# A state-space branch's diagonal part with two heads side by side, its other parts turned into the same bank

## The chip, the cores and the metric

The kernel runs on one core of a Trainium2 chip, in one launch. The metric is the device time of one execution in microseconds; the number shown for a kernel is the median over its runs. Beside the timed runs there is one profiled execution, from which every instruction's start and length on each engine are known. The engines are named as in the profile: PE multiplies matrices (PEld is its loading of the operand that stays in the array), DVE is the vector engine, ACT the scalar engine, POOL the general one, and SP issues DMAs. All operands are 32 bits wide. A tile of PSUM, into which PE writes, is a bank of 128 partitions by 512 numbers.

## The reference

One layer of a diffusion backbone over 512 latent tokens of width 1024, with 256 context tokens ahead of it. An adaLN-modulated RMSNorm feeds one combined input projection, whose columns go to two parallel mixers (a bidirectional state-space scan, and windowed attention with context keys) and to two gates. Each branch is projected to the model's width, the two are merged under the gates, projected once more and added to the stream; then comes a gated feed-forward part with a convolution. The part that the change touches is the scan's output, per chunk of 128 tokens and per direction:

```
cb = einsum('bclgn,bcsgn->bgcls', cc, bc)
scores = cb[:, :, None] * exp(segsum(ac))
y_diag = einsum('bgrcls,bcsgrp->bclgrp', scores, xc)
y_off = einsum('bclgn,bcgrpn,bgrcl->bclgrp', cc, states[:, :-1], exp(cs))
y = y_diag + y_off
...
y = y + d_skip * xs
return rmsnorm(y * silu(z), g)
```

There are 32 heads of 64 channels in 4 groups of 8 heads, and 4 chunks; the state has 128 numbers per channel. The norm runs over all 2048 channels and is followed by the projection with `w_o_ssd`.

## The kernel before

The kernel is written with a framework that places semaphores and buffers. Within a stretch it keeps the engines' instructions near program order; inside `manual_schedule` they stand exactly in it. The stages follow one another: modulation and the first columns of the gates (to about 64 us), keys, first queries and values (to 104), attention with z columns and further products beside it, in an order that a planner works out (to about 377), the state-space branch (to about 746), output projections (to about 905), and the feed-forward part (up and down products). Products of large weights are taken in three passes of split operands (`gemm`, L187); the branch's own small products are taken in plain 32-bit form, which is two matmuls each.

**The branch** (L1232 to L1509) is a list of steps, `prog`, that `run` (L167) goes through. For each of the 4 groups of heads there are the steps of `ssd_steps(g)` and, between them, projection steps of the next group (`proj_steps(g + 1)`), whose large products fill PE; for the last group the steps between are gate products (`g_step`). `run` loads each step's weights one step ahead.

- `proj_steps` (L1272): the group's B, C and four x tiles, each from a product with the latent tokens and mostly one with the context, then convolution and silu on ACT and DVE. Tiles that must be turned wait in a list, and the next step turns them between its two products (`turn`, L1262): a bank of PSUM per tile, transposes on PE, a copy out on ACT.
- `states` (L1365): the context's states and the backward states. Their pieces are put into the large products (`BETWEEN`).
- `chunk_in(c)` (L1404): loads two blocks of cumulated decays, multiplies C with B (`cb`, L1418), and makes `E`, the decayed scores of 8 heads, in two halves of four: ACT writes the backward part into a bank `eb` (L1436), DVE merges it into the forward part (L1437), ACT takes the exponential, DVE multiplies with `cb` (L1439). `E` lies with source tokens on partitions and output tokens along the free dimension.
- `chunk_out(c)` (L1442): C times the forward and the backward state (L1448), scaled on DVE (L1450) into `parts`. Then the diagonal part: one product per head into its 64 columns of the bank `yd` (L1454), with `E` staying in the array and 64 columns of `xs` streaming, so that tokens are on partitions. POOL adds up the skip term and the two parts in `dx` (L1459 to L1461), DVE adds `yd` and `dx` into `y` (L1462). Then the forward state advances (L1357 to L1360).
- `gate_rows` (L1466), just before the group's last `chunk_in`: loads four tiles of 128 channels by 512 tokens of silu(z), which attention had written to `zs_d`.
- `gate` (L1472), after the last chunk: for each of the four channel tiles, four transposes of `y` into a bank (L1479), a product with the gate rows on DVE (L1480), a store to `yz_d`. The rows' squares are summed for the norm during the next group (`square`, L1323).

In the branch all small products share one pool of five PSUM banks (`misb`, L1229): C times state (two), `yd`, the state's advance, `cb`, two `eb`, turned tiles, the gate's transposes.

**Modulation steps** (`m_step`, L543): the second half of the modulation (w_mod, 32 pieces of 512 KB) isn't multiplied on PE. Each step does two multiply-adds of 128 x 512 on DVE (L554 to L556), and each fourth step ends with four transposes on PE and a sum on DVE (L564 to L567), or for the last two with one product with ones and a sum (L559, L560). Steps 0 to 3 stand around the values' step at L688, steps 4 to 11 in the branch, two per group, 12 to 23 among the output projections, and 24 to 31 woven among the 22 up steps (L2021).

**After the branch**, `y_split` (L1521) loads the 16 tiles of `yz_d` again, multiplies by the norm's weights and splits them into high and low halves for the product with `w_o_ssd` (`os_first`, L1561, for the first two output tiles, pieces os 0 to 3; `os_step` for the others, two pieces each). `load` (L154) casts a weight piece into one of two buffers for the high and two for the low halves, unless `ELSEWHERE` names another place. The last up step takes its second bank from `misb`; then the banks are laid out anew as one pool of eight (`one_pool`, L2005), and the down products begin (L1868).

Products that are only 32 columns wide stand at L359 and L417, in the modulation: their outputs lie in 32 partitions each, four (three) after one another in one bank.

Of the kernel before, what the change touches and what calls it, by code (L numbers as in the profile page):

```python
# [9 lines left out]
F32 = mybir.dt.float32  # L10
# [34 lines left out]
def tile_hybrid_layer(  # L45
# [641 lines left out]
    msteps = [m_step(i) for i in range(32)]  # L687
    run([q_step(1)] + msteps[0:2] + [([("v", i) for i in range(3)], v_step)] + msteps[2:4])  # L688
# [547 lines left out]
    bp = bpool.enter_context(tc.tile_pool(name="bpool", bufs=1, reuse_waits="tile"))  # L1236

# [102 lines left out]
    def ssd_steps(g):  # L1340
# [24 lines left out]
        def states():  # L1365
# [36 lines left out]
            d["y"] = bp.tile([P, 4, 512], F32, tag="y", name="y", bufs=1)  # L1402
# [39 lines left out]
        def chunk_out(c):  # L1442
            xs, y, coef = d["xs"], d["y"], d["coef"]
# [8 lines left out]
            yd = misb()  # L1452
            for h in range(8):
                T.matmul(  # L1454
                    yd[:, h * 64 : (h + 1) * 64], d["E"][h // 4][:, h % 4, :], xs[:, c, h * 64 : (h + 1) * 64],
                    start=True, stop=True,
                )
            dx = bp.tile([P, 512], F32, tag="tf", name="dx", bufs=1)
# [3 lines left out]
            V.tensor_tensor(y[:, c, :], yd, dx, ALU.add)  # L1462
# [3 lines left out]
        def gate_rows():  # L1466
            for ct in range(4):
                zt = bp.tile([P, L], F32, tag="zs", name="zs", bufs=4)
                nc.sync.dma_start(zt, zs_d[4 * g + ct])
                d.setdefault("zt", []).append(zt)  # L1470

        def gate():  # L1472
            y = d["y"]
            if g == 0:
                dump("y", y[:, 1, :])
            for ct, yz in enumerate(d["zt"]):
                ps = misb()
                for c in range(4):
                    T.transpose(ps[:, c * P : (c + 1) * P], y[:, c, ct * P : (ct + 1) * P], ident)  # L1479
                V.tensor_tensor(yz, ps, yz, ALU.mult)  # L1480
                nc.sync.dma_start(yz_d[4 * g + ct], yz)
                SQUARES.append(yz)
                if g == 3:
                    square(False)

        r = [([], states)]
        for c in range(4):
            r += [([], lambda c=c: chunk_in(c)), ([], lambda c=c: chunk_out(c))]
        r[7] = [], lambda f=r[7][1]: (gate_rows(), f())
        return r + [([], gate)]  # L1490

    prog = proj_steps(0)
    for g in range(4):
# [3 lines left out]
        m = msteps[4 + 2 * g : 6 + 2 * g]  # L1497

        prog += s[0:1] + f + b[0:1] + s[1:2] + m[0:1] + b[1:2]
        for c in range(4):  # L1500
            prog += s[2 + 2 * c : 4 + 2 * c] if c < 3 else s[8:9]
# [3 lines left out]
            if c == 1:  # L1505
# [606 lines left out]
```

## Time and profile before

| | before |
|---|---|
| median of 3 runs | 1255.09 us (1254.44 to 1257.48) |
| the profiled execution's own time | 1254.76 us |
| its span, first to last instruction | 1253.0 us |
| PE / PEld busy | 1228.1 / 1010.6 us |
| DVE / ACT / POOL busy | 922.4 / 683.4 / 166.9 us |
| PE's granted clock, mean | 0.996 |

A row of the timeline gives start, length, engine, line, operation, output and inputs, the part of the array that is used (128*128 is all of it), shape, and how many instructions were merged; in brackets stands idle time of the engine just before, and what ended it. A group row gives busy time, mean length in ns, idle time before, and its releasers. PE's matmuls are pipelined: a row's length reaches to the end of the last matmul's way through the array, and the next matmul starts before that.

### The profile page before, as it was taken

Reading aid. Unit: us, or ns where it says so; the run is one execution under the profiler, and the core shown is the slowest. Engines: PE = TensorE matmul, PEld = TensorE weight load, DVE = VectorE, ACT = ScalarE, POOL = GpSimd, SP = SyncE. Lnnn points to the kernel's source line nnn. Section 1 sums busy time; section 2 is a strip of 40 time slices with the busy share of each in tenths; the row PEclk is TensorE's granted clock in tenths of the full one; section 3 lists DMA queues with packets and bytes.
Section 4 is the critical chain, followed back from the end, with each engine's and each line's share of the span. In section 5 each row is a group of like instructions: output and inputs, shape, how many; then the busy total and the mean of one; then the engine's idle time right before and its main releaser. Section 6 shows DMA issues by size and latency. Waiting matters only on the chain. (4 is left out here: it accounts for less than half of the span.)

```text
span 1253.0 us, 17432 instructions
## 1 busy us (share of the span) xinstructions
PE 1228.1 (98%) x6292; PEld 1010.6 (81%) x6292; DVE 922.4 (74%) x1517; ACT 683.4 (55%) x1286; POOL 166.9 (13%) x173
## 2 busy tenths in 40 slices
PE   7999999999999999999999999999999999999997
PEld 4698888888878878788778777888988888887885
DVE  4775888888664688788877767667678888886566
ACT  3566887788544456476565655223545444444543
POOL 0000111112100033242352520000200000000000
PEclk9899999999999999999999999999999999999999
DMA  9573568967946234345365549667145444458785
GB/s 340 220 214 103 185 191 202 227 177 197 245 146 206 74 115 123 126 129 174 112 143 175 160 154 308 219 220 235 58 143 168 152 134 151 149 165 276 228 308 184
DMA packets 109494, 226.74 MB, mean 181 GB/s; under 512 B 9568, under 2 KB 48800, under 8 KB 109408
## 3 DMA queue, kind: packets, MB, share of 16 engines
q1 hardware_dynamic: 101920, 199.42, 49.3%
q0 software_dynamic: 6912, 25.17, 8.6%
q8 instruction: 49, 0.80, 0.3%
q10 hardware_dynamic: 576, 1.05, 0.2%
q14 instruction: 37, 0.30, 0.1%
HBM read 194.34 MB, written 50.92 MB: 196 GB/s over the span
## 5 line engine op out<-in xcount | busy, mean ns | idle before, releaser
L150 DVE TENSOR_TENSOR wlo<-wraw,whi 128x1024 fp32r<-128x1024 f32 (+2 forms) x121 | 152.7, 1262 | 64.8 <-ACT whi L149 61.9
L193 PE MATMUL acc<-hlh,whi 128*128 128x512 f32 x488 | 200.1, 410 | 0.0
L196 PE MATMUL acc<-hlh,wlo 128*128 128x512 f32 x488 | 191.3, 392 | 0.0
L194 PE MATMUL acc<-hll,whi 128*128 128x512 f32 x488 | 190.8, 391 | 0.0
L149 ACT CAST whi<-wraw 128x1024 fp32r<-128x1024 f32 (+2 forms) x121 | 124.9, 1034 | 119.5 <-PE acc L194 72.3
L193 PE MATMUL acc<-mh,whi 128*128 128x512 f32 x360 | 140.6, 390 | 0.0
L194 PE MATMUL acc<-ml,whi 128*128 128x512 f32 x360 | 140.1, 389 | 0.0
L196 PE MATMUL acc<-mh,wlo 128*128 128x512 f32 x360 | 140.1, 389 | 0.0
L196 PEld LDWEIGHTS acc<-hlh,wlo 128*128 128x128 f32 x488 | 91.6, 188 | 20.1
L194 PEld LDWEIGHTS acc<-hll,whi 128*128 128x128 f32 x488 | 91.9, 188 | 18.1 <-issue 2.4
L193 PEld LDWEIGHTS acc<-hlh,whi 128*128 128x128 f32 x488 | 91.9, 188 | 17.7 <-issue 2.4
L194 PEld LDWEIGHTS acc<-ml,whi 128*128 128x128 f32 x360 | 67.6, 188 | 14.2 <-issue 0.2
L193 PEld LDWEIGHTS acc<-mh,whi 128*128 128x128 f32 x360 | 67.6, 188 | 14.1 <-issue 0.2
L196 PEld LDWEIGHTS acc<-mh,wlo 128*128 128x128 f32 x360 | 67.6, 188 | 14.1
L794 DVE CUSTOM_DVE_ANT_0 p<-score,winm,nsink 128x512 f32<-128x512 f32 (+1 forms) x64 | 51.9, 810 | 16.2 <-PE score L785 14.7
L801 ACT ACTIVATE p<-p,mneg 128x512 f32<-128x512 f32 (+1 forms) x64 | 49.7, 777 | 16.9 <-DVE mneg L794 16.4
L1240 DVE SCALAR_TENSOR_TENSOR ta<-acc,half,ta 128x511 f32<-128x511 f32 (+1 forms) x66 | 43.8, 663 | 18.9 <-ACT ta L1239 18.8
L1239 ACT ACTIVATE ta<-acc,half 128x512 f32<-128x512 f32 (+1 forms) x66 | 46.6, 705 | 20.4 <-PE acc L196 19.1
L193 PE MATMUL acc<-hch,whi 128*128 128x256 f32 x176 | 54.4, 309 | 0.0
L829 DVE TENSOR_TENSOR ptl<-pt,pth 128x512 fp32r<-128x512 f32 x72 | 47.5, 685 | 8.5 <-ACT pth L825 7.7
L1359 POOL TENSOR_TENSOR st<-st,eT 128x512 f32<-128x512 f32 x24 | 28.5, 1186 | 177.5 <-ACT st L1376 158.6
L556 DVE SCALAR_TENSOR_TENSOR tm<-wraw,csil,tm 128x512 f32<-128x512 f32 x56 | 41.9, 748 | 11.0 <-DMA wraw<-wm 10.1
(477 smaller groups left out, 2960.7 us busy)
## 6 DMA issues: line engine op xcount, KB each, us to landing
wraw<-wup SPq DMA_DIRECT2D x44, 512.0 KB, 3.8
wt_d<-wdn POOLq DMA_DIRECT2D x36, 512.0 KB, 7.7
wraw<-wm SPq DMA_DIRECT2D x32, 512.0 KB, 3.6
fb<-cs_d SPq DMA_DIRECT2D x32, 512.0 KB, 5.6
wraw<-wx SPq DMA_DIRECT2D x24, 512.0 KB, 3.7
wraw<-wt_d SPq DMA_DIRECT2D x20, 512.0 KB, 4.5
sp_d<-te SPq DMA_DIRECT2D x33, 256.0 KB, 2.4
wm<-wm SPq DMA_DIRECT2D x16, 512.0 KB, 8.0
```

The source lines that it names most:

```text
L149: S.copy(hi[:, :n], r[:, :n])
L150: V.tensor_tensor(lo[:, :n], r[:, :n], raw(hi[:, :n]), ALU.subtract)
L193: T.matmul(ps, wh, xh[:, k0 + k, :], start=a, stop=False)
L194: T.matmul(ps, wh, xl[:, k0 + k, :], start=False, stop=False)
L196: T.matmul(ps, wl, xh[:, k0 + k, :], start=False, stop=b)
L556: V.scalar_tensor_tensor(acc, r[:, u * 512 : u * 512 + 512], sc, acc, ALU.mult, ALU.add)
L794: V.tensor_tensor_reduce(p[:, :w], d["ps"][i][:, o0 : o0 + w], m, op0=ALU.add, op1=ALU.min, scale=1.0, scalar=nsink[:, h : h + 1], accum_o ...
L801: S.activation(p, p, AF.Exp, bias=d["mneg"][:, i : i + 1], scale=-1.0, accum_out=d["den"][:, i : i + 1])
L829: V.tensor_tensor(d["ptl"][x], d["pt"][x], raw(d["pth"][x]), ALU.subtract)
L1239: S.activation(o[:, :n], ps[:, :n], AF.Identity, scale=hcol(base_w, stride + i), bias=hcol(base_b, i))
L1240: V.scalar_tensor_tensor(o[:, 1:n], ps[:, 0 : n - 1], hcol(base_w, i), o[:, 1:n], ALU.mult, ALU.add)
L1359: G.tensor_tensor(h8(n), h8(s), bc64(eT[:, z0 : z0 + 8, c]), ALU.mult)
```

## The change

Seven things are changed.

1. The diagonal part is taken the other way round: 64 columns of `xs` stay in the array and a head's `E` (128 columns) streams, so that channels come out on partitions. The outputs of an even and an odd head lie in partitions 0 to 63 and 64 to 127 of the same 128 columns of a bank `yb`.
2. DVE no longer adds `dx`. A new step `chunk_sum(c)`, which stands after the next projection step (for the last group's first three chunks after the next `chunk_out` and `chunk_in`), turns the four column blocks of `dx` with PE and adds them into the same bank.
3. `chunk_sum` then multiplies the bank with the chunk's columns of the gate rows, in place in `z`, a tile for all four channel tiles with two buffers, loaded at the start of the group in `states`. `gate` has only the stores and the squares left; the tile `y` is gone.
4. The last group's rows aren't stored and loaded again: `y_split` reads them from `z`.
5. Modulation steps 0 to 3 move from the values' step into the branch, which then has three per group; the last eight are woven among the first 20 up steps instead of all 22.
6. The halves of weight piece os 4 go into a buffer of the pool of `z` instead of the common ones.
7. For odd chunks of the last group `dx` lies in another buffer.

```
-    msteps = [m_step(i) for i in range(32)]
-    run([q_step(1)] + msteps[0:2] + [([("v", i) for i in range(3)], v_step)] + msteps[2:4])
+    run([q_step(1), ([("v", i) for i in range(3)], v_step)])
...
+    zpool = ExitStack()
+    zp = zpool.enter_context(tc.tile_pool(name="zpool", bufs=1, side="right", reuse_waits="tile"))
...
-            d["y"] = bp.tile([P, 4, 512], F32, tag="y", name="y", bufs=1)
+            d["z"] = zp.tile([P, 4, L], F32, tag="z", name="z", bufs=2)
+            for ct in range(4):
+                nc.sync.dma_start(d["z"][:, ct, :], zs_d[4 * g + ct])
...
-            yd = misb()
+            yb = misb()
             for h in range(8):
                 T.matmul(
-                    yd[:, h * 64 : (h + 1) * 64], d["E"][h // 4][:, h % 4, :], xs[:, c, h * 64 : (h + 1) * 64],
-                    start=True, stop=True,
+                    yb[64 * (h % 2) : 64 * (h % 2) + 64, h // 2 * P : h // 2 * P + P],
+                    xs[:, c, h * 64 : (h + 1) * 64], d["E"][h // 4][:, h % 4, :],
+                    start=h < 2, stop=False, skip_group_check=True,
                 )
-            dx = bp.tile([P, 512], F32, tag="tf", name="dx", bufs=1)
+            dx = tmp("tc") if g == 3 and c % 2 else bp.tile([P, 512], F32, tag="tf", name="dx", bufs=1)
+            d["y", c] = yb, dx
...
-            V.tensor_tensor(y[:, c, :], yd, dx, ALU.add)
             if c < 3:
                 d["Sf"] = advance(d["Sf"], 0, c, weigh_in(0, c))

-        def gate_rows():
+        def chunk_sum(c):
+
+            yb, dx = d.pop(("y", c))
             for ct in range(4):
-                zt = bp.tile([P, L], F32, tag="zs", name="zs", bufs=4)
-                nc.sync.dma_start(zt, zs_d[4 * g + ct])
-                d.setdefault("zt", []).append(zt)
+                z = slice(ct * P, (ct + 1) * P)
+                T.matmul(yb[:, z], dx[:, z], ident, start=False, stop=ct == 3, is_transpose=True, skip_group_check=True)
+            z = d["z"][:, :, c * P : (c + 1) * P]
+            V.tensor_tensor(z, yb.rearrange("p (a b) -> p a b", a=4), z, ALU.mult)

         def gate():
-            y = d["y"]
...
-            for ct, yz in enumerate(d["zt"]):
-                ps = misb()
-                for c in range(4):
-                    T.transpose(ps[:, c * P : (c + 1) * P], y[:, c, ct * P : (ct + 1) * P], ident)
-                V.tensor_tensor(yz, ps, yz, ALU.mult)
-                nc.sync.dma_start(yz_d[4 * g + ct], yz)
+            for ct in range(4):
+                yz = d["z"][:, ct, :]
                 SQUARES.append(yz)
-                if g == 3:
+                if g < 3:
+                    nc.sync.dma_start(yz_d[4 * g + ct], yz)
+                else:
                     square(False)
+            F["z"] = d["z"]
...
-        m = msteps[4 + 2 * g : 6 + 2 * g]
+        m = msteps[3 * g : 3 * g + 3]
...
         for c in range(4):
-            prog += s[2 + 2 * c : 4 + 2 * c] if c < 3 else s[8:9]
+            prog += s[3 * c + 2 : 3 * c + 3] + (s[3 * c + 4 : 3 * c + 5] if c < 3 else [])
+            if g == 3 and c:
+                prog += s[3 * c : 3 * c + 1]
             prog += b[2 + c : 3 + c]
             if c == 1:
                 prog += b[6:]
-            if c == 1:
-                prog += m[1:2]
-        prog += s[9:10]
+            if g < 3 or c == 3:
+                prog += s[3 * c + 3 : 3 * c + 4]
+            if c in (1, 2):
+                prog += m[c : c + 1]
+        prog += s[13:14]
...
-            t = tmp("ta") if k < 3 else ldt[k % 3] if k % 6 < 3 else cp.tile([P, L], F32, tag="ld", name="ld", bufs=3)
-            nc.sync.dma_start(t, yz_d[k])
+            if k < 12:
+                t = tmp("ta") if k < 3 else ldt[k % 3] if k % 6 < 3 else cp.tile([P, L], F32, tag="ld", name="ld", bufs=3)
+                nc.sync.dma_start(t, yz_d[k])
+            else:
+                t = F["z"][:, k - 12, :]
...
+    def second_piece():
+        t = zp.tile([P, 2, 1024], F32R, tag="z", name="z", bufs=2)
+        return t[:, 0, :], t[:, 1, :]
+
+    ELSEWHERE["os", 4] = second_piece
...
-        + weave([up_step(t) for t in range(NFF)], msteps[24:])
+        + weave([up_step(t) for t in range(NFF - 2)], msteps[24:])
+        + [up_step(t) for t in range(NFF - 2, NFF)]
```

More of the change, by code (lines that the diff above doesn't have):

```diff
@@ L1442, in chunk_out @@
         def chunk_out(c):
-            xs, y, coef = d["xs"], d["y"], d["coef"]
+            xs, coef = d["xs"], d["coef"]
             tok = slice(c * P, (c + 1) * P)
@@ L1712, in close_c1 @@
         c1pool.close()
+        zpool.close()
         c2 = F["c2"] = ctx.enter_context(tc.tile_pool(name="c2pool", bufs=1, reuse_waits="tile"))
```

6 lines of the change are left out of this document (2 added, 4 removed).

## The prediction

> **What bounds the kernel now.** I read the page's busy shares first, then the list of PE's waits, then the busy time of each engine over the branch's first group (window from, to, length; then PE, PEld, DVE, ACT, POOL), then the timeline of PE around the diagonal part.
>
> ```profile
> PE 1228.1 (98%) x6292; PEld 1010.6 (81%) x6292; DVE 922.4 (74%) x1517; ACT 683.4 (55%) x1286; POOL 166.9 (13%) x173
> ```
>
> ```profile
> PE mis L1267 <- DVE y L1462: 0.5, 1, 0.5
> ```
>
> ```profile
> 440.00:506.00 66.00, 65.90 (x363) 52.93 (x362) 56.11 (x89) 42.83 (x105) 25.36 (x17) 1.00 0.37 111
> ```
>
> PE is busy for 98% of the span, and in that group for 65.90 of 66.00 us; DVE, next, has 56.11. So an edit is worth what it takes off PE's own stream, plus the few places where PE stands still. An edit on DVE, ACT, POOL or a queue counts only if it uncovers PE.
>
> **The diagonal part.** Here are one chunk, the group of all sixteen, and the one place where the kernel before already puts products side by side in the array: the modulation products, 32 columns wide, four across.
>
> ```profile
> 467.80 1.88 PE L1448 MATMUL mis<-st,CT 128*128 128x512 f32 x4
> 469.51 1.89 PE L1454 MATMUL mis<-xs,E 128*128 128x64 f32 x16
> 471.25 1.08 PE L1357 MATMUL mis<-xw,Bk 128*128 128x512 f32 x2
> ```
>
> ```profile
> L1454 PE MATMUL mis<-xs,E 128*128 128x64 f32 x256 | 31.1, 274 | 0.7 <-DVE E L1439 0.7
> ```
>
> ```profile
> 13.80 0.84 PE L408 MATMUL mis<-ah,w0l 128*128 128x512 f32 x2
> 14.58 1.07 PE L359 MATMUL acc<-wm,csil 128*32 128x256 f32 x16
> 15.58 0.73 PE L408 MATMUL mis<-ah,w0h 128*128 128x512 f32 x2
> 16.15 0.62 PE L408 MATMUL mis<-al,w0h 128*128 128x512 f32 x2
> ```
>
> ```profile
> L193 PE MATMUL acc<-mh,whi 128*128 128x512 f32 x360 | 140.6, 390 | 0.0
> ```
>
> ```profile
> 14.57 0.59 PEld L359 LDWEIGHTS acc<-wm,csil 128*32 128x32 f32 x16 [0.44 <-issue]
> ```
>
> A product of f32 operands is two matmuls, so eight heads are 16 matmuls. Now they take 471.25 - 469.51 = 1.74 us, 0.109 each. The operand that streams is only 64 wide: four matmuls of 512 columns take 469.51 - 467.80 = 1.71, or 0.428 each, and 64 columns by that are 0.054. So PE is held by the loading of E, 128 columns per matmul. Over all chunks the group is 31.1 busy + 0.7 idle, less 0.15 sixteen times (a row of 1.89 whose successor starts after 1.74): 29.4 us.
>
> After the change xs is loaded (64 columns) and E streams (128 columns, 0.107 by the same rate), with even heads in the left half of the array and odd heads in the right. If the halves run at once, a chunk is 8 x 0.107 = 0.86. What entering and leaving a divided array costs, I take from the modulation row. The second L408 matmul before it starts at 13.80 + 0.84 - 0.39 = 14.25 (0.39 is one matmul of 512 such columns, by the group row; a pair of 0.62 says that they come 0.23 apart); the next was due at 14.48. Afterwards two L408 matmuls precede 16.15, so with no loss they would have begun at 16.15 - 2 x 0.23 = 15.69. That is 1.21 for 16 matmuls of 256 columns, four at once: 4 x 0.214 = 0.86. The visit costs 0.35 beside its streaming. I take 0.86 + 0.35 = 1.21 per chunk, 19.4 in all: **-10.0 us**. Ends: no cost of the visit, 13.8 (-15.6); halves that don't overlap, 16 x 0.107 + 0.35 = 2.06 per chunk, 33.0 (+3.6). I stay near the row of the divided array, since it is the same element type and the same bank for all quarters.
>
> The 16 transposes per group stay 16, only of dx instead of y and four per chunk:
>
> ```profile
> L1479 PE MATMUL mis<-ident,y 128*128 128x128 f32 x64 | 7.6, 272 | 0.0
> ```
>
> ```profile
> 477.86 0.82 PE L1267 MATMUL mis<-ident,tc 128*128 128x128 f32 x6
> ```
>
> Each lasts 0.27, and in a run of only six they come (0.82 - 0.27) / 5 = 0.11 apart, all that their 128 columns stream for, so making four runs of four out of one run of sixteen costs nothing.
>
> **DVE in the branch.**
>
> ```profile
> L556 DVE SCALAR_TENSOR_TENSOR tm<-wraw,csil,tm 128x512 f32<-128x512 f32 x56 | 41.9, 748 | 11.0 <-DMA wraw<-wm 10.1
> ...
> L1462 DVE TENSOR_TENSOR y<-mis,dx 128x512 f32<-128x512 f32 x16 | 11.1, 692 | 24.6 <-POOL dx L1461 24.6
> L1480 DVE TENSOR_TENSOR zs<-mis,zs 128x512 f32<-128x512 f32 x16 | 10.4, 682 | 1.0 <-PE mis L1479 1.0
> ```
>
> The sums of L1462 go: 11.1 busy, and the 24.6 for which DVE stood in front of them for POOL, with the next chunk's E queued behind. The gate products stay 16 of 128x512. Four modulation steps come in: 8 x 0.75 = 6.0, and by the group's 11.0 idle for 56, some 1.6 of waiting for their 512 KB rows. DVE gains near 28 us here, so I cost the steps at nothing; E also comes sooner. With L1462 gone, the 0.5 that L1267 waited goes: **-0.5**. The gate rows' 16 loads move on SP from chunk 3 to the group's start, past the weight loads, and those wait only if a row buffer (two groups deep) is still being squared; the last group's 4 stores and 4 loads go. PE waits for none of these loads: nothing. Were that cover gone, a weight load would come late by one landing of 256 KB, 2.4 us, once per group at most:
>
> ```profile
> sp_d<-te SPq DMA_DIRECT2D x33, 256.0 KB, 2.4
> ```
>
> **The places where PE stands.**
>
> ```profile
> 103.92 0.60 PE L564 MATMUL mis<-ident,tm 128*128 128x128 f32 x4
> 105.60 0.39 PE L785 MATMUL score<-khi,q 128*128 128x256 f32 x1 [1.08 <-DVE mod L566]
> ```
>
> ```profile
> 771.75 1.05 ACT L149 CAST whi<-wraw 128x1024 fp32r<-128x1024 f32 x1 [1.99 <-PE acc L194]
> ...
> 775.45 1.22 DVE L150 TENSOR_TENSOR wlo<-wraw,whi 128x1024 fp32r<-128x1024 f32 x1
> ...
> 776.72 0.50 PE L196 MATMUL acc<-yh,wlo 128*128 128x512 f32 x1 [1.67 <-DVE wlo L150]
> ```
>
> ```profile
> 1133.34 1.02 PE L559 MATMUL mis<-tm,ones 128*128 128x512 f32 x2
> ...
> 1135.01 0.68 DVE L560 TENSOR_TENSOR g<-mis,g 128x512 f32<-128x512 f32 x1
> 1135.61 0.74 DVE L1762 SCALAR_TENSOR_TENSOR tc<-mis,vec,tc 128x511 f32<-128x511 f32 x1
> 1135.84 0.47 PE L1868 MATMUL acc<-ww,fyh 128*128 128x512 f32 x1 [1.48 <-DVE g L560]
> ```
>
> Front: the first score waits 1.08 for the modulation step's bank (L566). That step leaves; its four transposes (0.44) are paid in the branch instead. Next late is the evacuation of the v banks, running since 102. I take **-1.1** (ends -1.1 and 0).
>
> Output weights: the piece for os 4 can be cast only when os 1's buffer is free (771.75), and its low half stands on DVE behind the merges, until 776.67; PE waits 1.67. In buffers of its own both halves can be made as soon as the piece has landed: **-1.7** (ends -1.7, and 0 if DVE keeps its order).
>
> Down: PE waits 1.48 for the last modulation step's bank. Two up steps earlier that step (its 0.85 on PE too) is out of the way, but the last up product's bank is then read until about 1135.7 by L1762 instead. If the first down bank is that one, the wait stays and the 0.85 comes on top; if the second, six matmuls run first and some 1.0 of waiting is left; else it is gone. With one of five banks for each of the first two: 0.2 x 0.85 - 0.2 x 0.5 - 0.6 x 1.5 = **-0.8** (ends -1.5, +0.85).
>
> New waits: the diagonal's bank is now held through the following projection until chunk_sum's product, in a pool of five in which that step turns two tiles and E holds three:
>
> ```profile
> 477.94 0.73 DVE L1437 COPY_PREDICATED E<-sel,mis 128x512 f32<-128x512 uint8 x1
> ...
> 479.97 0.74 DVE L1437 COPY_PREDICATED E<-sel,mis 128x512 f32<-128x512 uint8 x1
> ```
>
> With the turn at 477.86, cb, both E banks and the two turned tiles are five; the held bank is a sixth. The second tile starts at 478.30 and would wait for the first copy, done at 478.67. In this chunk L1462 came before that copy and had waited for POOL 1.19, which goes, so I take the copy as early enough, mostly: **+1.0** over the 12 projection steps (ends 0 and +8.9, below).
>
> Sum: -10.0 - 0.5 - 1.1 - 1.7 - 0.8 + 1.0 = -13.1. The profiled execution took 1254.76 (span 1253.0 and 1.8 around it): 1241.7. The median of the runs, 1255.09, is 0.3 above: **1242.0**. A measurement can tell some 0.3%, 3.8 us, from no change.
>
> **The rivals.**
>
> In order: the two halves start strictly in the program's order, so a head's second pass holds up its neighbour and a chunk is nine rounds, +0.107 x 16 = 1.7: 1243.7. Against it:
>
> ```profile
> 32.85 0.41 PE L417 MATMUL acc<-w,s 128*32 128x256 f32 x3
> 32.89 0.40 PE L359 MATMUL acc<-wm,csil 128*32 128x256 f32 x1
> 33.00 0.48 PE L417 MATMUL acc<-w,s 128*32 128x128 f32 x3
> ```
>
> L417's products all stand ahead of L359's in the program, yet one of L359, in the fourth quarter, starts at 32.89 before the last of L417 at 33.00. The Trainium skill, "TensorE: Matmul & The Clock Gate", Part 3, says that matmuls start and end strictly in program order; by that rule the time would be this rival's, and these rows disagree with it. 6%.
>
> Loads not hidden: each half loads, then streams. One load lasts 0.106 for 32 columns and 0.19 for 128:
>
> ```profile
> L359 PEld LDWEIGHTS acc<-wm,csil x128: 106/110/178, 6.2 to 53.2; 128*32 128x32 f32 x128
> ```
>
> ```profile
> L1454 PEld LDWEIGHTS mis<-xs,E x256: 186/192/192, 456.5 to 738.2; 128*128 128x128 f32 x128
> ```
>
> Between them 64 columns are 0.134, and 8 x (0.134 + 0.107) + 0.35 = 2.28 per chunk, 36.5: +7.1 in place of -10.0, so 1259.1, **slower**. It decides once a load's exposed part passes 0.08. The 16 loads of the modulation row, done within 0.59 while its matmuls run 1.07, speak against it. The same Part 3 says that loads overlap running matmuls only in other row groups, which would make this rival right here; the row disagrees. 5%.
>
> No overlap of the halves: +3.6 in place of -10.0 gives 1255.6, no change. The four quarters at 14.58 speak against it. 6%.
>
> Banks, short: the 0.37 above (478.67 - 478.30) at each turn, and as much again at the next chunk's C product, which needs the held bank's successor: 12 x 0.74 = 8.9 in place of 1.0, 1249.9. For it: the five banks are all taken at 477.86. 8%.
>
> Banks, long: the second turned tile is given the bank of E's second copy, done at 480.71: 2.4 x 12 = 28.9 in place of 1.0, 1269.9, slower. It decides from 1.5 per turn. 5%.
>
> **How the numbers follow.** The forecast has the other 70%. Faster: 70 + 6 + 8 = 84%; same: 6%; slower: 5 + 5 = 10%. The range runs from the visit without cost (-15.6 for -10.0: 1236.4, rounded to 1236.5) up to the short bank waits, 1250.0; outside are 16% in rivals and little below.
>
> **What would show it.** Right: the diagonal as 128*64 matmuls of 128x128, about 1.2 us per chunk from its first start to the next group's; no L1462 among DVE's groups; PE's waits at the score, at os 4's low half and at the first down product gone or smaller; turns of a tile with no idle time before them. Wrong: chunks of over 1.8 us; PE waiting at the turns for a copy of E or for ACT; E late at the diagonal, at more than the 0.7 of before.

## The result and the profile after

| | before | after |
|---|---|---|
| median of 8 runs each | 1255.55 us (1253.54 to 1257.48) | 1251.16 us (1249.31 to 1252.82) |
| the profiled execution's own time | 1254.76 us | 1249.31 us |
| its span | 1253.0 us | 1247.3 us |
| PE / DVE busy | 1228.1 / 922.4 us | 1220.3 / 919.5 us |

The ratio is 0.9965, 95% interval 0.9954 to 0.9976: 4.4 us faster where 13.1 were forecast. The profiled execution after is the fastest of its eight; of the 5.7 by which the spans differ, 1.0 was there before the first product of the gates, ahead of every edited step.

The diagonal came out as forecast. The timeline of PE after, for the chunk of the prediction (start, length, then the operation), and its group:

```profile
463.89 0.60 PE L1475 MATMUL mis<-ident,dx 128*128 128x128 f32 x4
464.32 1.88 PE L1451 MATMUL mis<-st,CT 128*128 128x512 f32 x4
466.14 1.09 PE L1457 MATMUL mis<-E,xs 128*64 128x128 f32 x16
467.16 1.12 PE L1358 MATMUL mis<-xw,Bk 128*128 128x512 f32 x2
468.12 0.38 PE L1421 MATMUL mis<-CT,BT 128*128 128x128 f32 x2
```

```profile
L1457 PE MATMUL mis<-E,xs 128*64 128x128 f32 x256 | 17.9, 280 | 0.3 <-DVE E L1442 0.2
```

From the first start to the next group: 467.16 - 466.14 = 1.02, where it was 1.74. The group ahead lasts 1.82 in place of 1.71 and the one behind 0.96 in place of 0.91, so the visit to the divided array costs 0.16 more around it: 1.18 per chunk against the forecast 1.21, 0.56 saved, 9 us in all. The front's wait and the down product's wait are gone too; the first score and the first down product have no bracket now:

```profile
102.89 0.28 PE L784 MATMUL score<-khi,q 128*128 128x256 f32 x1
...
1130.53 0.39 PE L1885 MATMUL acc<-ww,fyh 128*128 128x512 f32 x1
```

What was not forecast is in the list of PE's waits (us in total, times, longest). In the branch the kernel before had, beside the 0.5 that the prediction shows:

```profile
PE mis L1454 <- DVE E L1439: 0.7, 2, 0.4
PE mis L1267 <- DVE tc L1248: 0.3, 1, 0.3
```

After the change these lines are new or longer:

```profile
PE acc L193 <- ACT whi L149: 2.5, 1, 2.5
PE acc L196 <- DVE wlo L150: 1.2, 1, 1.2
PE mis L1451 <- ACT xs L1311: 1.2, 1, 1.2
PE mis L1268 <- DVE tc L1249: 1.0, 2, 0.8
PE mis L1268 <- DVE E L1440: 0.9, 2, 0.7
...
PE mis L1358 <- DVE z L1477: 0.7, 1, 0.7
```

The last four lie in the branch, where the list now adds up to 4.5 us (0.7 of it in three short lines) and to 1.5 before. The first two lie where the branch ends. The timeline of PE there:

```profile
743.54 0.39 PE L196 MATMUL acc<-hlh,wlo 128*128 128x512 f32 x1
746.43 0.50 PE L193 MATMUL acc<-yh,whi 128*128 128x512 f32 x1 [2.50 <-ACT whi L149]
...
748.37 0.50 PE L196 MATMUL acc<-yh,wlo 128*128 128x512 f32 x1 [1.21 <-DVE wlo L150]
...
749.18 0.63 PE L196 MATMUL acc<-yh,yh 128*128 128x512 f32 x1
749.60 0.63 PE L193 MATMUL acc<-yh,whi 128*128 128x512 f32 x1
```

PE stands for 2.50 and 1.21 us, and then its matmuls of 512 columns come 0.42 to 0.43 apart instead of 0.23. The brackets are somewhat short: they count from the end of the row before, so where 743.54 is followed by 746.43, 2.89 later in place of 0.23, the loss is 2.66. The windows of those stretches (after the length: busy PE, PEld, DVE, ACT, POOL, then the granted clock) show why:

```profile
746.00:749.00 3.00, 1.36 (x5) 0.84 (x6) 3.00 (x4) 1.81 (x3) 0.00 (x0) 1.00 0.98 328
749.00:752.00 3.00, 3.00 (x9) 2.37 (x8) 1.15 (x2) 0.00 (x0) 0.00 (x0) 0.53 0.79 263
```

The granted clock fell to 0.53; it was 1.00 throughout there before. (A window from 749.16 to 752.57 has exactly 0.50: 3.41 us at half speed, which is 1.7 lost.) And this is what ACT did meanwhile, which PE waited for, the cast of weight piece os 0 (L149, at 745.35):

```profile
736.14 2.93 ACT L1536 ACTIVATE yh<-ld,vec 128x512 fp32r<-128x512 f32 x4 [1.21 <-DMA ld<-yz_d]
...
742.55 1.93 ACT L1536 ACTIVATE yh<-ld,vec 128x512 fp32r<-128x512 f32 x3
744.72 0.72 ACT L1536 ACTIVATE yh<-ld,vec 128x512 fp32r<-128x512 f32 x1 [0.24 <-DMA ld<-yz_d]
745.35 1.03 ACT L149 CAST whi<-wraw 128x1024 fp32r<-128x1024 f32 x1
```

In the kernel before, the same cast had stood ahead of the squares and of all the splits (L1526 there):

```profile
743.85 1.05 ACT L149 CAST whi<-wraw 128x1024 fp32r<-128x1024 f32 x1 [5.80 <-PE acc L194]
...
747.63 1.94 ACT L1526 ACTIVATE yh<-ta,vec 128x512 fp32r<-128x512 f32 x3
```

After the change it stands behind the first twelve of the gated rows' splits (L1536), in the order of ACT's queue. The piece's load was issued at 716.60, and the product whose buffer the cast takes over was done at 737.8, before L1475 turns the last chunk.

Where the time went is best read by comparing the start of the same matmul in two timelines, stage by stage. Each number is how much longer (+) or shorter (-) the stage took than in the kernel before, in us of the profiled executions; the front begins at the first product of the gates (63.58 in the kernel before), and the stages end there at 106.18 (first gate product after the scores), 391.98, 745.54 (start of the last gate product), 781.84 (behind the first two output tiles and piece os 4), 1135.84 (first down product) and 1253.0.

| kernel | front | attention | branch | first output tiles | output, up | down |
|---|---|---|---|---|---|---|
| the change | -1.8 | -0.5 | -4.1 | +4.0 | -1.9 | -0.4 |
| e1 stored | -1.8 | -0.4 | -2.6 | +3.3 | -1.9 | -0.4 |
| e2 seam split | -1.8 | -0.4 | -0.5 | -1.9 | -1.9 | -0.3 |
| e3 six banks throughout | -1.8 | -0.4 | -7.0 | +4.9 | +4.3 | -0.4 |
| e4 steps in front | 0.0 | -0.4 | -7.7 | -1.9 | -1.9 | +1.0 |
| e5 second and third step earlier | -1.8 | -0.5 | -2.0 | -1.9 | -1.9 | +0.1 |
| e6 none in last group | -1.8 | -0.4 | -5.7 | -1.9 | -1.4 | -0.4 |
| e7 four steps later | -1.8 | -0.4 | -7.5 | -1.9 | +1.5 | -0.4 |
| e8 heads' order | 0.0 | -0.4 | -2.9 | -1.9 | -1.9 | -0.4 |
| e9 one step late | 0.0 | -0.5 | -7.0 | +4.5 | +0.8 | +1.3 |
| e10 six banks in the branch | -1.8 | -0.4 | -6.1 | +4.5 | -1.9 | +0.7 |
| e11 three in front | -1.8 | -0.4 | -4.6 | -1.9 | -1.9 | +0.3 |
| e12 three in front, six banks | -1.8 | -0.4 | -9.6 | -1.9 | -1.9 | +0.2 |
| e13 steps moved alone | -1.8 | 0.0 | +3.2 | +0.9 | -2.4 | 0.0 |
| e14 without two edits | 0.0 | -0.5 | -7.7 | -2.1 | -2.3 | +0.2 |

So the change lost in two places: in the branch it gained 4.1 of the 9 that its diagonal is worth, and at the first output tiles it lost 4.0, though os 4's wait of 1.67, in the same stage, is gone: 5.7 in all, which is the two waits with what their brackets leave out (2.66 and 1.37) and the 1.7 of the clock.

### The profile page after: what moved, and what is told of

It is laid out like the page before. It is cut to its first block, busy times and chain, and to the rows that moved or that the text cites. A ratio compares the mean times of both kernels' runs of the same rounds, so it can differ in the third digit from the quotient of the medians.

```text
span 1247.3 us, 17416 instructions
## 1 busy us (share of the span) xinstructions
PE 1220.3 (98%) x6292; PEld 994.3 (80%) x6292; DVE 919.5 (74%) x1501; ACT 685.9 (55%) x1286; POOL 164.1 (13%) x173
## 4 chain that ended last, share of the span: by engine, by line
PE 83%; DVE 10%; ACT 2%; issue 2%; DMA 2%; POOL 1%; SPq 0%; POOLq 0%; DVEq 0%; ACTq 0%
PE acc L196 17%; PE acc L193 17%; PE acc L194 17%; PE acc L1887 3%; PE acc L1885 3%; PE acc L1886 3%; PE score L784 3%; PE po L833 3%; PE pt L820 2%; PE mis L408 2%; DVE wlo L150 1%; PE acc L903 1%; PE acc L905 1%; PE acc L904 1%; PE mis L1375 1%
## 5 line engine op out<-in xcount | busy, mean ns | idle before, releaser
L150 DVE TENSOR_TENSOR wlo<-wraw,whi 128x1024 fp32r<-128x1024 f32 (+2 forms) x120 | 149.9, 1250 | 70.0 <-ACT whi L149 61.8
L193 PE MATMUL acc<-hlh,whi 128*128 128x512 f32 x488 | 200.2, 410 | 0.0
L149 ACT CAST whi<-wraw 128x1024 fp32r<-128x1024 f32 (+2 forms) x120 | 123.9, 1034 | 117.6 <-PE acc L194 78.1
L193 PE MATMUL acc<-mh,whi 128*128 128x512 f32 x360 | 141.0, 392 | 0.0
L193 PEld LDWEIGHTS acc<-hlh,whi 128*128 128x128 f32 x488 | 91.8, 188 | 18.3 <-issue 2.9
L193 PEld LDWEIGHTS acc<-mh,whi 128*128 128x128 f32 x360 | 67.6, 188 | 14.5 <-issue 0.5
L193 PE MATMUL acc<-hch,whi 128*128 128x256 f32 x176 | 54.4, 309 | 0.0
L556 DVE SCALAR_TENSOR_TENSOR tm<-wraw,csil,tm 128x512 f32<-128x512 f32 x56 | 44.5, 794 | 13.3 <-DMA wraw<-wm 12.8
```

Source lines behind the costliest of these rows:

```text
L149: S.copy(hi[:, :n], r[:, :n])
L150: V.tensor_tensor(lo[:, :n], r[:, :n], raw(hi[:, :n]), ALU.subtract)
L193: T.matmul(ps, wh, xh[:, k0 + k, :], start=a, stop=False)
L556: V.scalar_tensor_tensor(acc, r[:, u * 512 : u * 512 + 512], sc, acc, ALU.mult, ALU.add)
```

## The experiments

Each is timed beside the kernel before on the same chip, and ratios are to that kernel. The chip isn't the same one for all, so it is the ratios that compare one experiment with another. "The change" is 0.9965.

| kernel | median us | ratio, 95% interval |
|---|---|---|
| e1 | 1248.63 | 0.9963 (0.9951 to 0.9976) |
| e2 | 1246.49 | 0.9936 (0.9923 to 0.9948) |
| e3 | 1253.73 | 0.9991 (0.9982 to 1.0001) |
| e4 | 1241.75 | 0.9903 (0.9889 to 0.9916) |
| e5 | 1246.64 | 0.9929 (0.9916 to 0.9941) |
| e6 | 1241.88 | 0.9901 (0.9886 to 0.9916) |
| e7 | 1243.44 | 0.9906 (0.9892 to 0.9919) |
| e8 | 1245.71 | 0.9928 (0.9915 to 0.9942) |
| e9 | 1253.12 | 0.9984 (0.9973 to 0.9995) |
| e10 | 1248.16 | 0.9952 (0.9939 to 0.9966) |
| e11 | 1242.45 | 0.9907 (0.9893 to 0.9920) |
| e12 | 1238.54 | 0.9873 (0.9859 to 0.9886) |
| e13 | 1254.22 | 0.9999 (0.9990 to 1.0008) |
| e14 | 1241.72 | 0.9893 (0.9879 to 0.9906) |

The first theory was that the end of the branch suffers because the last group's stores are gone from SP; its rival, that the held bank costs what is missing.

**e1: the last group's rows stored and loaded again.**

```
-                if g < 3:
-                    nc.sync.dma_start(yz_d[4 * g + ct], yz)
-                else:
+                nc.sync.dma_start(yz_d[4 * g + ct], yz)
+                if g == 3:
                     square(False)
...
```

> The change as it is, but the last group's four gated tiles are stored and loaded again like the others. Seam theory (without those four stores on SP the split of the gated rows is issued and worked off ahead of os 0's weight piece, so that PE runs dry for 2.50 + 1.21 us at the end of the branch and then gets a lower clock): the old order comes back, PE runs on from the last gate projection into the first output product without idle time, and the time falls by 4 to 6 us below the change, to about 1246. Bank theory (the shortfall is PE's waiting in the branch for a bank that the diagonal holds): the seam is indifferent, within 1 us of the change, about 1251. Prediction's step (those stores and loads are worth nothing): about 1251 too.

The ratio is that of the change, and PE still waited 1.77 and 1.34 us at the first output products. The theory in this form falls: removing those stores and loads is not what made the stall.

**e2: eight of the sixteen splits put behind the first output products.**

```
-        [([], lambda: y_split(range(12)))]
-        + fill[n3:]
-        + [os_first(0), ([], lambda: y_split(range(12, 16))), os_first(1)]
+        [([], lambda: y_split(range(4)))]
+        + fill[n3:]
+        + [([], lambda: y_split(range(4, 8))), os_first(0), ([], lambda: y_split(range(8, 16))), os_first(1)]
```

> The change as it is, but only tiles 0 to 3 of the gated rows are split ahead of the last gate projection, 4 to 7 behind it, 8 to 15 behind os 0 and os 2; stores and loads stay away. Seam theory: os 0's cast comes before the last splits, the wait of 2.50 at the first output product goes, 4 to 6 us below the change, about 1246. Bank theory: within 1 us of the change.

The stall is gone, and the stage of the first output tiles went from +4.0 to -1.9: 5.9 us, as expected for the order of ACT's queue. But the branch, which the edit doesn't name, kept only 0.5 of its 4.1, so the median shows half of it. Its list of waits in the branch is 2.5 us longer than the change's: for turned tiles (DVE tc, 2.5 in place of 1.0) and for E (two lines, 1.0 more). Why DVE is later there I didn't find out.

**e3 and e10: six banks for the branch's products, two for its projections**, throughout (e3), or in the branch alone (e10, which has the second part of the edit too).

```
-    psum_pools(mis=(5, 1), acc=(3, 1))
+    psum_pools(mis=(6, 1), acc=(2, 1))
...
     run(prog)
+    psum_pools(mis=(5, 1), acc=(3, 1))
     bpool.close()
```

> The change with six banks for the branch's products and two for the projections, in place of five and three. Bank theory: PE's waits in the branch for a copy of E, a turned tile or the gate product (0.9, 1.0, 1.0 and 0.4 us in the change) go, 2 to 3 us below the change, about 1248.5, unless two projection banks bring waits of their own at the projections (then slower, and those waits show in the list at the projection matmuls). Seam theory: the wait of 2.50 at the end of the branch stays; no more than 1 us gained. Modulation theory (the waits come from four more modulation steps on DVE): waits stay, no gain.

> The change with six banks for the branch's products and two for its projections, put back to five and three when the branch ends. Bank theory: the branch gains some 2.9 us as it did with six and two throughout, and the output and feed-forward stages lose nothing now: 2 to 3 us below the change, 1248 to 1249. Place theory: the waits at the end of the branch (2.50 and 1.21) stay, and the 5.8 us there. If the gain in the branch was chance, 1251.

The branch gained 2.9 and 2.0 more than in the change. The list of PE's waits of e10 in the branch has lost the gate product's lines and the turns' wait for a copy of E, and has a new one for the two projection banks (L193):

```profile
PE acc L193 <- DVE ta L1242: 1.5, 2, 1.0
PE mis L1268 <- DVE tc L1249: 1.2, 3, 0.9
...
```

In e3 the output stages then lost 6.2 with two banks (+4.3 for -1.9), more than the branch had won; e10 keeps its gain, 1.6 us below the change by the ratios. The stall at the end stays in both (2.22 and 1.48 in e3, 2.1 and 1.1 in e10). So one bank more takes away a part of the loss in the branch and nothing at its end. The kernel before was not tried with six and two, so how much of that part is the bank that the diagonal holds stays open.

**e4: the four modulation steps back in front.**

```
-    run([q_step(1), ([("v", i) for i in range(3)], v_step)])
+    msteps = [m_step(i) for i in range(32)]
+    run([q_step(1)] + msteps[0:2] + [([("v", i) for i in range(3)], v_step)] + msteps[2:4])
...
-    msteps = [m_step(i) for i in range(32)]
...
-        m = msteps[3 * g : 3 * g + 3]
+        m = msteps[4 + 2 * g : 6 + 2 * g]
```

> The change with its first four modulation steps back ahead of the attention, two per group in the branch as before. Modulation theory (DVE is late in the branch because of the added steps): PE's waits in the branch fall from 4.5 us to 1.5 or less and 1.8 us of transposes leave it, while the front loses 1.5 to 2: 2 to 3 us faster than the change, about 1248.5. Bank theory: the waits in the branch stay at 3.5 or more, and front and branch cancel: within 1 us of the change. Seam theory: the 2.50 at the end of the branch stays.

The time is 1241.75: the largest effect of all, 0.6% below the change, and more than the modulation theory asked for. PE's whole list from 60 us on:

```profile
PE mis L1269 <- DVE E L1441: 1.2, 2, 0.7
PE score L785 <- DVE mod L566: 1.1, 1, 1.1
PE mis L1359 <- DVE z L1478: 0.7, 1, 0.7
PE mis L1269 <- DVE tc L1250: 0.3, 2, 0.2
```

The branch's waits fell from 4.5 to 2.2, and the stall at its end is gone, with nothing edited there. The timeline of ACT (e4) shows os 0's cast ahead of the squares and the last splits:

```profile
736.30 1.04 ACT L149 CAST whi<-wraw 128x1024 fp32r<-128x1024 f32 x1
...
738.34 0.62 ACT L1335 ACTIVATE tc<-z 128x512 f32<-128x512 f32 x1
...
740.43 2.55 ACT L1536 ACTIVATE yh<-ld,vec 128x512 fp32r<-128x512 f32 x4
```

A new theory follows, in two forms: the four steps cost by their place (the last group's third step, at chunk 2, stands so late that it turns ACT's order round) or by their number.

**e5 and e6: the same twelve steps, each group's second at chunk 0 and its third at chunk 1** (e5); **none in the last group, three more among the output steps** (e6).

```
-            if c in (1, 2):
-                prog += m[c : c + 1]
+            if c < 2:
+                prog += m[c + 1 : c + 2]
```

```
-        m = msteps[3 * g : 3 * g + 3]
+        m = msteps[3 * g : 3 * g + 3] if g < 3 else []
...
-        + weave([os_step(o) for o in range(3, 8)], msteps[12:18])
+        + weave([os_step(o) for o in range(3, 8)], msteps[9:18])
```

> The change with the same twelve modulation steps in the branch, but each group's third step one chunk earlier (beside its second, at chunk 1, in place of chunk 2). Place theory (the third step of the last group, its reduction and its loads, stands so late that the split of the gated rows and os 0's cast are put in another order on ACT and PE runs dry at the end of the branch): the waits of 2.50 and 1.21 at the first output products go, the time falls by 4 to 6 us below the change, to about 1246. Amount theory (any twelve steps in the branch make DVE late): no more than 1 us below the change; the waits in the branch stay at 4 us or more in both.

> The change with three modulation steps in each of the first three groups, none in the last, and three more among the output steps. Place theory: the waits at the end of the branch go, and with them those of the last group on DVE's turned tiles (1.0): 5 to 7 us below the change, about 1245; groups 1 and 2 keep their waits of 1.2, 0.7 and 0.7. Amount theory: only about a quarter of the waits in the branch goes, 1 us. Bank theory: nothing but the last group's.

Both lose the stall (-1.9 in that stage), so the place decides about it. E6 is as fast as e4, faster than expected. The edit of e5 does more than its expectation says: the third step doesn't come beside the second at chunk 1, the second moves too, to chunk 0. E5 pays in the branch: the turns stand for DVE's copies of E, once for 2.66 us, and then the granted clock is 0.50 for a while (642.0 to 645.4).

```profile
PE mis L1268 <- DVE E L1440: 4.5, 4, 2.7
```

**e9: one step late.** The kernel of e4, in which only the last group's second step is put at chunk 2.

```
-            if c in (1, 2):
-                prog += m[c : c + 1]
+            if c == (2 if g == 3 else 1):
+                prog += m[1:2]
```

> The kernel with the four steps back in front (1241.75), with one thing moved: the last group's second modulation step, the one that reduces, stands at chunk 2 in place of chunk 1. Place theory: this single step puts os 0's cast behind the last splits, PE runs dry for some 3 to 4 us at the first output products, and 2 to 4 us more go in a lower clock: 4 to 6 us slower than 1241.75, 1246 to 1248. Amount theory (it is the number of steps): 1242, no wait at the first output products.

By the ratios (0.9984 - 0.9903) it is 10 us slower than e4, twice what was expected. PE's timeline (e9) has the stall again, and a second one at the first down product:

```profile
744.73 0.50 PE L193 MATMUL acc<-yh,whi 128*128 128x512 f32 x1 [2.64 <-ACT whi L149]
...
747.01 0.50 PE L196 MATMUL acc<-yh,wlo 128*128 128x512 f32 x1 [1.55 <-DVE wlo L150]
...
1131.87 0.47 PE L1885 MATMUL acc<-ww,fyh 128*128 128x512 f32 x1 [2.53 <-DVE tc L1779]
```

On ACT the cast is back behind the splits, at 743.65:

```profile
741.20 2.55 ACT L1536 ACTIVATE yh<-ld,vec 128x512 fp32r<-128x512 f32 x4
743.65 1.03 ACT L149 CAST whi<-wraw 128x1024 fp32r<-128x1024 f32 x1
```

The stage of the first output tiles goes from -1.9 to +4.5, 6.4 us; the wait for the bank that the last up product's L1779 reads is 2.53 more, with a lower clock behind it. So one step of the same work, moved by one chunk, makes the stall. How the framework's placing of instructions comes to turn the order by it, these runs don't show.

**e7 and e11: the four steps elsewhere.** Two per group in the branch and four more among the output steps (e7); three in front and the fourth, which transposes and reduces, in the first group (e11, shown against e4).

```
-        m = msteps[3 * g : 3 * g + 3]
+        m = msteps[2 * g : 2 * g + 2]
...
-        + weave([os_step(o) for o in range(3, 8)], msteps[12:18])
-        + weave([out_step(o) for o in range(5)], msteps[18:24])
+        + weave([os_step(o) for o in range(3, 8)], msteps[8:16])
+        + weave([out_step(o) for o in range(5)], msteps[16:24])
```

```
-    run([q_step(1)] + msteps[0:2] + [([("v", i) for i in range(3)], v_step)] + msteps[2:4])
+    run([q_step(1)] + msteps[0:2] + [([("v", i) for i in range(3)], v_step)] + msteps[2:3])
...
-        m = msteps[4 + 2 * g : 6 + 2 * g]
+        m = msteps[3:6] if g == 0 else msteps[4 + 2 * g : 6 + 2 * g]
```

> The change with none of the four steps ahead of the attention and two per group in the branch, the other four among the output steps. If the front's gain (1.6 to 1.8) and the branch's gain (about 8, without the four added steps) both hold, this is 1.6 us below the kernel with the four steps back in front (1241.75): about 1240. If the steps cost the same wherever they stand, about 1246 to 1248.

> Three of the four steps back in front, the fourth, which transposes and reduces, in the branch's first group. The wait of 1.08 before the first score and 0.44 of transposes belong to the fourth step alone, so the front keeps its gain of 1.6; one step more in the first group costs 0.44 and little else, and none stands late in the last group: 1.0 to 1.5 us below the kernel with all four in front (1241.75), about 1240.5. By the amount theory each step in the branch costs about 2: about 1242.

Both missed by the gain: each keeps the front's 1.8 and pays more than that elsewhere (e7: 3.4 in output and up; e11: 3.1 in the branch against e4, for one step). Neither differs from e4 beyond the interval. All of e11's 3.1 is lost in its first group, by the starts of the same products. The change has three steps in that group too (steps 0 to 2, none of which reduces) and loses nothing against e4 there; it loses 1.8 in the second group, where its step 3 reduces, 0.9 in the third and 0.9 behind it. So the price doesn't go by the number of steps. That it is the reducing step, which also takes one of the five banks for its transposes, is likely by this and not shown alone.

**e12: e11 with the banks of e10.**

> The last kernel together with six and two banks in the branch, five and three behind it. If what is left of PE's waits in the branch (some 2 us, on E's copies and on the gate product) is the bank that the diagonal holds, 1.5 to 2 us below the last kernel, about 1239; if six and two only changed the order of other things, no more than 0.5 below it.

1238.54, the fastest kernel here, 3.9 below e11 (timed together), twice what was expected. Of e11's 4.0 us of waits in the branch these are left:

```profile
PE acc L193 <- DVE ta L1243: 0.5, 1, 0.5
PE mis L1269 <- DVE tc L1250: 0.3, 2, 0.2
PE mis L1458 <- DVE E L1443: 0.2, 1, 0.2
```

and the branch shows -9.6, so there is room in it for the diagonal's whole 9.

**e8: heads 0, 2, 4, 6, 1, 3, 5, 7** on the kernel of e4.

```
-            for h in range(8):
+            for h in (0, 2, 4, 6, 1, 3, 5, 7):
```

> The kernel with the four steps back in front (1241.75), its diagonal's eight products issued in the order of heads 0, 2, 4, 6, 1, 3, 5, 7: first all of the left half, then all of the right half. Rival of the strict order (a matmul starts only after the one ahead of it in the program has started): the right half's first product waits for the left half's last start, 7 x 0.107 = 0.75, then 0.86 more: 1.6 us per chunk in place of 1.02, about 9 us in all, 1251. If each half takes its own products as they come, whatever their order: 1.02 per chunk stays, 1242. If the halves ran one after the other: the same as now.

The diagonal's chunk in e8 and in e4, with its successor:

```profile
467.71 1.58 PE L1458 MATMUL mis<-E,xs 128*64 128x128 f32 x16
469.22 1.13 PE L1359 MATMUL mis<-xw,Bk 128*128 128x512 f32 x2
```

```profile
467.35 1.09 PE L1458 MATMUL mis<-E,xs 128*64 128x128 f32 x16
468.37 1.12 PE L1359 MATMUL mis<-xw,Bk 128*128 128x512 f32 x2
```

1.51 in place of 1.02, so the order of the heads matters, by 0.49 x 16 = 7.8 us of PE (4.8 in the branch; the list of waits there has 0.3 left of e4's 2.2). But it is neither of the two cases. The windows of that line in e8 (PE's matmuls that run in each stretch, in brackets, PEld's loads behind):

```profile
467.70:468.18 0.48, 0.47 (x4) 0.47 (x5) 1.00 0.51 157
468.18:468.58 0.40, 0.40 (x9) 0.40 (x8) 1.00 0.50 128
468.58:469.06 0.48, 0.48 (x10) 0.47 (x5) 1.00 0.30 85
```

At first the left half runs alone, then both, then the right alone. In the trace's single records the matmuls of one half start 0.109 apart; the right half's first starts 0.493 after the chunk's first, some 0.006 after the fifth of the left half's eight, and the left half's last starts only at 0.815. All sixteen chunks show this, within 0.002. So it doesn't wait for all that precede it, as strict order would have it (7 x 0.109 = 0.76), nor start at once. The Trainium skill ("TensorE: Matmul & The Clock Gate", Part 3) has matmuls start and end strictly in the program's order; these records disagree. They look like a limited look ahead: the right half's first starts when three of those ahead of it in the program have not.

**e13: the modulation moved alone**, in the kernel before (the diffs of e4, read backwards, and the third slot at chunk 2). **e14: e4 without the buffers for os 4 and without the earlier last modulation steps** (the edit against e4, without the lines of `second_piece` itself).

```
-    ELSEWHERE["os", 4] = second_piece
...
-        + weave([up_step(t) for t in range(NFF - 2)], msteps[24:])
-        + [up_step(t) for t in range(NFF - 2, NFF)]
+        + weave([up_step(t) for t in range(NFF)], msteps[24:])
```

> The kernel before with nothing changed but the modulation: four steps out of the front, three per group in the branch, at the change's places. If the twelve steps in the branch cost by themselves (DVE has less idle time here than in the change, since it still waits 24.6 us for POOL), PE gets new waits in the branch of 3 us or more, and the time is 1254.5 less 1.6 for the front plus 3 or more: 1256 or above. If they cost only together with the rest of the change (the early split of the gated rows, the held bank), the branch keeps its waits of about 1.2, os 0's cast keeps its early place, and the front's gain is left: about 1253.

> The diagonal side by side with its accumulation and the gate rows in place, the last group's rows kept on chip, but the four modulation steps in front, no buffers of its own for os 4, and the last modulation steps among the last up products as before. By the prediction's terms: 1.74 - 1.17 = 0.57 per chunk, 9.1, and 0.5 at the turn, less 1 to 2 of new waits in the branch: 8 us below the kernel before, about 1246.5; the waits of 1.67 at os 4 and of 1.48 at the first down product are back. If the side by side diagonal brought less than its rows say, 1250 or above.

e13: no change that shows. The front gains its 1.8 and the branch loses 3.2, so the steps cost there by themselves. PE's list in its branch:

```profile
PE mis L1453 <- DVE E L1438: 0.9, 2, 0.6
PE mis L1266 <- DVE y L1461: 0.4, 1, 0.4
PE mis L1266 <- DVE tc L1247: 0.4, 1, 0.4
PE mis L1447 <- ACT xs L1309: 0.2, 1, 0.2
```

That is 1.9 in place of 1.5, so the list names only 0.4 of the 3.2, and the four transposes are 0.44. By the starts of the matmuls, the turns take 1.1 us more in all and C's products 0.9 more, with a bracket or without; what ended the waits without a bracket isn't shown. There is no stall at the branch's end, where os 0's cast had its old place on ACT. That stall needs both, the late step and the rest of the change. e14 missed in the other direction: it is as fast as e4, the two edits are worth nothing, and the waits of 1.67 and 1.48 don't come back without them.

## Why the prediction was wrong

**The step that failed** is this sentence of "DVE in the branch": "DVE gains near 28 us here, so I cost the steps at nothing". It summed DVE's gain over the branch, but PE waits for single instructions of DVE, at places: for the turned tiles (L1249), the copies of E (L1440), the gate product (L1477). Four steps more put 0.75 us pieces, reductions and their order ahead of those. Measured: 3.2 us in the branch of the kernel before (e13), 3.6 in the change (-7.7 against -4.1); of the 3.6, the list of waits shows 2.3 (4.5 for 2.2). One of the prediction's own signs of being wrong came true with it: PE waits at the turns for a copy of E, 0.9. Nor did the prediction name what is queued behind a late step at the branch's end: os 0's cast, whose turn on ACT it changed, 5.9 us with the lower clock. With the front's 1.8 set against it, the move costs 3.6 + 5.9 - 1.8 = 7.7; by the ratios, 0.9965 - 0.9903, 7.8. (Between the two profiled executions it is 1.4 less, since e4's down stage is longer by that; why isn't shown.) Without the move the change is 1241.75, close to the forecast, and in part by luck: its branch gains 7.7 where the forecast's terms for it come to 9.5, and the two stages behind it 3.8 where 2.5 was forecast, not for the reasons given.

**The diagonal** was right: 1.18 per chunk for 1.21, and e12's branch of -9.6 has room for all of its 9 us. Both halves run at once, and no load shows.

**The front** was right in the wait and small in size: -1.8 for -1.1, the wait of 1.08, the four transposes (0.44, which I set against their place in the branch), and some 0.3.

**New bank waits** were mis-sized: +1.0 forecast. Six banks in the branch gave back 2.0 (e10) and 5.0 (e12 against e11 in that stage). If all of that is the held bank, which wasn't shown apart from the steps' own need of banks, the term was between 2 and 5, inside its ends of 0 and 8.9.

**The last group's stores and loads at nothing** was right (e1). My first reading of the stall, that they had held the splits back, was not.

**os 4 and down** had the right sizes for the wrong reason. The waits are gone, but in e14 they are gone without the two edits. Os 4's is 2.58 in e13, so it went with the diagonal or the rows kept on chip; which of the two wasn't tried. The down wait went in e13, where the up steps stand as before, and came back in e9 with the edit in place: there the first down product was handed the bank that the last up product's L1779 reads, the case that the prediction gave 0.2, and the place of the last step didn't prevent it.

**Left open**: about 1.5 us of the change's branch (9 for the diagonal, less 3.0 of waits, 4.5 for 1.5 before, and 0.44 of transposes, is 5.6; 4.1 was measured) that no line of the list names. The brackets explain a part: each is some 0.16 short, as at 743.54, and nine stand in the change's branch for four before, an estimate of 0.8. Open too: why DVE is later in e2's branch.

## What to carry over

Cover for a moved step is not the idle total of its engine but the slack of the next instruction on that engine that the bound engine waits for; look at each place where the step lands, above all at the last one before a stage changes. Where a scheduler places instructions, a step moved by one chunk can reorder a queue far from it, so compare the order of the queues at the seams first. When a product is held in a bank longer, count the pool again: here one bank more, taken from the projections, took 1.6 us off the change (e10, by the ratios) and 3.9 off e11 (e12).

## What the runs showed of the hardware

After the change's two gaps of 2.50 and 1.21 us, within 4.5 us, came 3.41 us at a granted clock of 0.50; after e10's of 2.15 and 1.09, 6.82 us of it. In e9 one gap of 2.53 was enough (0.57 in a stretch that began 2.1 us after it, 0.50 from 1133.14 to 1136.56), while in e13 one of 2.58 left the clock at 1.00. The windows of e9 and of e13:

```profile
1134.00:1137.00 3.00, 3.00 (x10) 2.33 (x9) 3.00 (x7) 1.96 (x5) 0.00 (x0) 0.57 0.88 271
```

```profile
778.00:781.00 3.00, 3.00 (x13) 2.45 (x14) 3.00 (x5) 0.49 (x2) 0.00 (x0) 1.00 0.84 277
```

So a wait of some 2.5 us can cost 1.7 more (e9), two that add up to 3.2 can cost 3.4 more (e10), and one of 2.58 nothing more (e13). The Trainium skill ("TensorE: Matmul & The Clock Gate", Part 1, "What's actually happening") puts the fall to half rate after at least one idle window of about 3.4 us that runs freely; the free running would fit these two unlike cases, but here 2.53 us were enough.

A divided array's two halves worked side by side from the start when their matmuls alternated in the queue (1.02 us for sixteen), and only for a part of the time when eight of one stood ahead of eight of the other (1.51).
